# A decoder layer at fp32 accuracy: seven more pairs of gemms through seven block products, and the mixer's constants loaded at other places

## Chip, cores and metric

The kernel runs on one core of one Trainium2 chip. The metric is the device time of one execution in microseconds (us). The profile has five engines: PE (TensorE, with its weight loads as PEld), ACT (ScalarE), DVE (VectorE), POOL (GpSimd) and SP (SyncE, which issues nearly all DMAs).

## The reference

One layer, x of 256 tokens × 2048, all in float32, batch 1:

```python
x = x + 1/2 * SwiGLU_1(rms(x))          # SwiGLU(x) = (silu(x @ w_gate) * (x @ w_up)) @ w_down, D_FF 5632
h = rms(x)
[q | k | v | u | vs | g_att | g_sg] = h @ w_in                # 1536 each for q k v u vs, 2048 each gate
# A: 12 heads of 128, causal dilated windows (128,1) (512,4) (2048,16), partial rotary -> y_att (w_att_out)
# B: u = gelu(u); vs = layernorm(gelu(vs)); y_sg = (u * (W_s vs + b)) @ w_sg_out, W_s lower triangular per group
merged = sigmoid(g_att) * y_att + sigmoid(g_sg) * y_sg
x = x + merged @ w_out
x = x + 1/2 * SwiGLU_2(rms(x))
out = rms(x)
```

## The kernel before

All gemms have 256 rows (two token tiles of 128) and are cut into column blocks of 512; `gemm(w, c0, rows0, nk, lhs, post, group, bank, quad)` puts one such block on a list. The left operand lies in SBUF turned (features on the partitions), the weights stream from HBM.

**Accuracy.** Operands are split into a high and a low part of a reduced type (fp32r): hi is a rounded copy, lo the rest. A product is three matmuls, hi·hi, hi·lo and lo·hi. Weights are split by ACT (L235, `wh`) and DVE (L236, `wl`), 128×1024 at a time.

**Steps.** The list of gemms becomes a list of steps (`lay_out`). A plain step is two rows of 128 of k: one `wh`, one `wl`, 12 matmuls of 128×512. Raw weights come in units of 1 MB (`load_unit`, L181), three buffers deep, each for two plain steps. The main loop issues the matmuls of step i (L243), then the callbacks that are due at its end, then the splits of up to three steps ahead (LA = 3); `wh` and `wl` have four buffers. The order on every engine is the order in which this loop writes the instructions, and an engine does its queue in that order. `at(place, fn)` registers a callback; places count plain steps as 1 and quad steps as 0.5.

**Quads.** Two gemms side by side can do one chunk of four k rows as a 2×2 by 2×2 block product with seven products instead of eight (`quad_products`, forms p1 to p7). Each form is a quad step: six matmuls, one `wh`, one `wl`. Four blocks of raw weights (512 KB each, `load_block`) sit in a room; `prepare` (L211) makes four sums and differences of them on DVE, `sums_of` (L311 to L317) those of the left operand, and three ACT copies and two DVE adds (L292 to L301) put the results together in PSUM. p1, p6 and p7 are done 5, 3 and 1 steps ahead of the end of the gemm before, the others among the first five steps of the pair. Before the change there are 27 quads: nearly all of FFN1 and FFN2. In FFN2 the first pair of gate and up (f = 0) is plain; so is the whole mixer. `CS = 2` is the chunk of x that quads take.

**Turns.** A result that becomes a left operand is turned by `turn`: DVE transposes of 32×32 (L349) into `bt`, a DMA to a buffer in HBM (`bm`, L333), four DMAs back (L339), then `ev`: for x, ACT scales it by the norm's gains (L430) and splits it into `xhi` (ACT, L321) and `xlo` (DVE, L322). For chunk 2 of x0 and x2 `sums_of` follows at once, with its ACT copy (L316) and its lo part (L317). The operands x0, x1, x2 (of FFN1, mixer, FFN2) have four chunks each (`xt1_0` to `xt1_3`: x1's).

**Residuals.** `residual` adds a gemm's result to x (DVE, L411), ACT sums the squares (L377), and the turn of that chunk follows.

**The mixer.** In order: vs and u (three gemms each, gelu, layer norm, the spatial products), q and k, v, attention among them; then for c = 0 to 3 the gate gs (w_in), w_sg_out, ga (w_in), w_att_out and the turn of merged chunk c; then w_out. `mixer_consts` loads the rope table `cs_t`, the attention masks, the spatial weights (`room`) and the layer norm's rows (`ln`), L526 to L546, nine steps ahead of the mixer; two `sgw_turn`s turn the spatial weights 8 and 18 steps into it.

Of the kernel before, what the change touches and what calls it, by code (L numbers as in the profile page):

```python
# [18 lines left out]
P = 128  # L19
# [19 lines left out]
CS = 2  # L39
# [5 lines left out]
def layer(ctx: ExitStack, tc: tile.TileContext, a, out):  # L45
# [138 lines left out]
    def next_of(quad):  # L184
        k = quads.index(quad) + 1
        return quads[k] if k < len(quads) and quads[k]["stage"] is quad["stage"] else None

    def room_for(quad):
        quad["room"] = (big.tile([P, 4, 2, NC], F32, tag="C", name="quads"), big.tile([P, 2, NC], F32, tag="k2", name="sum"),
                        sb.tile([P, 3, NC], F32, tag="W", name="part"))  # L190
        for b in (0, 2, 3, 1):
            load_block(quad, b)

    def load_block(quad, b):
        if quad is None:
            return
        if "room" not in quad:
            quad["room"] = quads[quads.index(quad) - 1]["room"]
# [3 lines left out]
        SP.dma_start(quad["room"][0][:, b], src[:, j])  # L202

    def blocks_of(quad):
        r = quad["room"]
        return [r[0][:, b] for b in range(4)] + [r[1], r[2][:, 1:3], r[2][:, 0]]
# [98 lines left out]
    def sums_of(tag_pool, tag, v, name):  # L305

        v = v.rearrange("p (q m) i b -> p m q i b", m=4)
        a0, a1, b0, b1 = (v[:, m] for m in range(4))
        f = sb.tile([P, 4, 2, P], F32, tag="gate", bufs=2, name=f"fs{name}")
        s1, s2, s3, s4 = (f[:, k].rearrange("p q (i b) -> p q i b", b=32) for k in range(4))  # L310
        DVE.tensor_tensor(s1, a1, b1, op=OP.add)  # L311
        DVE.tensor_tensor(s2, s1, a0, op=OP.subtract)
        DVE.tensor_tensor(s3, a1, a0, op=OP.subtract)
        DVE.tensor_tensor(s4, b0, s2, op=OP.subtract)
        both = tag_pool.tile([P, 2, 4, 2, P], F32R, tag=tag, name=f"fp{name}")
        ACT.activation(both[:, 0], f, AF.Copy)  # L316
        DVE.tensor_tensor(both[:, 1], f, both[:, 0].bitcast(F32), op=OP.subtract)  # L317
        return both[:, 0], both[:, 1]
# [107 lines left out]
    def turn_x(i, n, c, lag, read=3):  # L426
        def evac(src):
# [5 lines left out]
            if c == CS and n != 1:  # L433
                xT["forms"] = sums_of(big, "oT", src, f"x{n}")
# [235 lines left out]
    def post_qk(key, gi):  # L670
        def post(e, banks):
# [58 lines left out]
            if key == "k" and gi == 2:  # L730
                attention(e + 16)
# [374 lines left out]
```

## Time and profile before

| what | value |
|---|---|
| time, median of 3 runs (lowest, highest) | 2026.97 us (2026.89, 2029.02) |
| profiled execution: time, span, granted clock | 2025.94 us, 2024.2 us, 0.997 |
| instructions in it | 24110 |
| bytes moved, mean rate | 471.54 MB, 233 GB/s |
| DMA queue of SP, share of 16 engines | 71.9% |

A row of the groups reads: line, engine, operation, out<-in, shape, count | busy us, mean ns | idle just before, and its releaser. In the timeline the numbers ahead are the start and the duration in us, and brackets hold idle time and its releaser. Matmuls are pipelined, so that a single one's 0.38 us overlaps its neighbours.

### The profile page before, as it was taken

How to read it: one execution, taken by the hardware profiler on the slowest of the kernel's cores; microseconds unless marked ns; L12 is line 12 of the kernel's file. 1: busy time of each engine (PE TensorE's matmuls, PEld its weight loads, DVE VectorE, ACT ScalarE, POOL GpSimd, SP SyncE). 2: the span in 40 equal slices, each digit the busy share in tenths (PEclk: the TensorE clock that was granted, in tenths of full speed). 3: DMA queues.
4: the chain of work that ended last, by engine and by line, in shares of the span. 5: the costliest groups of instructions: out<-in, count | busy, mean ns of one | idle time of the engine just before them, and what ended most of it. 6: DMA issues, size and time to landing. Idle time of an engine off the chain costs nothing.

```text
span 2024.2 us, 24110 instructions
## 1 busy us (share of the span) xinstructions
PE 2002.4 (99%) x9323; PEld 1750.0 (86%) x9323; DVE 1437.0 (71%) x1463; ACT 1105.7 (55%) x1240; POOL 11.3 (1%) x19
## 2 busy tenths in 40 slices
PE   9999999999999899999999999999999999999998
PEld 7888888888888788888888888888888888888887
DVE  6788776778877567675665555677878776787775
ACT  6555645555556455454554444466655554566554
POOL 0000000000000000000000000000000000000000
PEclk9999999999999999999999999999999999999999
DMA  8778776677775876788776666788777766687764
GB/s 313 257 232 249 229 233 214 198 228 232 242 244 183 273 252 204 227 276 267 259 235 216 229 204 216 237 279 253 235 221 239 254 211 192 219 248 229 233 214 142
DMA packets 249499, 471.54 MB, mean 233 GB/s; under 512 B 12460, under 2 KB 41000, under 8 KB 249256
## 3 DMA queue, kind: packets, MB, share of 16 engines
q1 hardware_dynamic: 249064, 469.47, 71.9%
q8 instruction: 73, 1.20, 0.2%
q10 hardware_dynamic: 320, 0.53, 0.1%
q14 instruction: 42, 0.34, 0.1%
HBM read 440.30 MB, written 29.66 MB: 232 GB/s over the span
## 4 chain that ended last, share of the span: by engine, by line
PE 93%; DMA 2%; DVE 2%; ACT 1%; issue 1%; SPq 0%; POOLq 0%; POOL 0%; ACTq 0%; DVEq 0%
PE qd L243 57%; PE mm L243 35%; DMA xt<-bmx 1%; DMA more<-in_ffn_w_gate_dram 1%; DVE wl L236 1%; ACT xt L430 0%; ACT wh L235 0%; DMA raw<-in_ffn_w_down_dram 0%; DMA raw<-in_ffn_w_gate_dram 0%; ACT xhi L321 0%; DVE btx L349 0%; PE sp L646 0%; DMA bmx<-btx 0%; SPq L339 0%; PE pv L812 0%
## 5 line engine op out<-in xcount | busy, mean ns | idle before, releaser
L236 DVE TENSOR_TENSOR wl<-raw,wh 128x1024 fp32r<-128x1024 f32 (+1 forms) x665 | 806.9, 1217 | 411.1 <-ACT wh L235 409.3
L235 ACT ACTIVATE wh<-raw 128x1024 fp32r<-128x1024 f32 (+1 forms) x665 | 696.0, 1051 | 598.4 <-PE mm L243 300.8
L243 PE MATMUL qd<-wh,xhi 128*128 128x512 f32 x1026 | 388.9, 379 | 0.0
L243 PE MATMUL qd<-wl,xhi 128*128 128x512 f32 x1026 | 388.9, 379 | 0.0
L243 PE MATMUL qd<-wh,xlo 128*128 128x512 f32 x1026 | 388.9, 379 | 0.0
L243 PE MATMUL mm<-wh,xhi 128*128 128x512 f32 x928 | 352.6, 380 | 2.2 <-ACT wh L235 1.9
L243 PE MATMUL mm<-wh,xlo 128*128 128x512 f32 x928 | 351.8, 379 | 0.0
L243 PE MATMUL mm<-wl,xhi 128*128 128x512 f32 x928 | 350.0, 379 | 1.7 <-DVE wl L236 1.7
L243 PEld LDWEIGHTS qd<-wl,xhi 128*128 128x128 f32 x1026 | 193.9, 189 | 27.7
L243 PEld LDWEIGHTS qd<-wh,xhi 128*128 128x128 f32 x1026 | 193.9, 189 | 27.7
L243 PEld LDWEIGHTS qd<-wh,xlo 128*128 128x128 f32 x1026 | 193.9, 189 | 27.4
L243 PEld LDWEIGHTS mm<-wh,xhi 128*128 128x128 f32 x928 | 175.4, 189 | 27.8 <-ACT wh L235 2.8
L243 PEld LDWEIGHTS mm<-wl,xhi 128*128 128x128 f32 x928 | 175.4, 189 | 27.1 <-DVE wl L236 2.3
L243 PEld LDWEIGHTS mm<-wh,xlo 128*128 128x128 f32 x928 | 175.4, 189 | 25.0 <-DVE xlo L404 0.3
L235 ACT ACTIVATE wh<-quads 128x1024 fp32r<-128x1024 f32 x108 | 114.0, 1055 | 146.5 <-PE qd L243 141.6
L236 DVE TENSOR_TENSOR wl<-quads,wh 128x1024 fp32r<-128x1024 f32 x108 | 131.4, 1217 | 50.1 <-ACT wh L235 49.3
L243 PE MATMUL qd<-wh,fpx 128*128 128x512 f32 x304 | 102.9, 379 | 1.4 <-DVE qd L301 1.4
L236 DVE TENSOR_TENSOR wl<-sum,wh 128x1024 fp32r<-128x1024 f32 x54 | 66.1, 1225 | 37.0 <-ACT wh L235 35.3
L235 ACT ACTIVATE wh<-sum 128x1024 fp32r<-128x1024 f32 x54 | 57.1, 1057 | 29.2 <-PE qd L243 18.1
L243 PEld LDWEIGHTS qd<-wh,fpx 128*128 128x128 f32 x304 | 57.5, 189 | 9.9 <-ACT wh L235 1.8
L243 PE MATMUL qd<-wh,hhi23.0_663 128*128 128x512 f32 x172 | 65.2, 379 | 0.0
L243 PE MATMUL qd<-wl,hhi23.0_663 128*128 128x512 f32 x172 | 65.2, 379 | 0.0
(402 smaller groups left out, 2366.0 us busy)
## 6 DMA issues: line engine op xcount, KB each, us to landing
raw<-in_w_in_dram SPq DMA_DIRECT2D x92, 1024.0 KB, 5.3
raw<-in_ffn_w_down_dram SPq DMA_DIRECT2D x72, 1024.0 KB, 5.2
raw<-in_ffn_w_gate_dram SPq DMA_DIRECT2D x66, 1024.0 KB, 6.2
raw<-in_ffn_w_up_dram SPq DMA_DIRECT2D x66, 1024.0 KB, 5.8
quads<-in_ffn_w_gate_dram SPq DMA_DIRECT2D x38, 512.0 KB, 5.7
quads<-in_ffn_w_up_dram SPq DMA_DIRECT2D x38, 512.0 KB, 3.6
quads<-in_ffn_w_down_dram SPq DMA_DIRECT2D x32, 512.0 KB, 3.8
raw<-in_w_out_dram SPq DMA_DIRECT2D x16, 1024.0 KB, 5.1
```

The costliest lines, as they stand in the source:

```text
L235: ACT.activation(wh[:, k], r[:, k], AF.Copy)
L236: DVE.tensor_tensor(wl[:, k], r[:, k], wh[:, k].bitcast(F32), op=OP.subtract)
L243: PE.matmul(g["ps"][t], act, in_turn(w), start=not g["begun"][t], stop=g["left"][t] == 0, skip_group_check=g["quad"] is not None)
```

## The change

- Seven more pairs become quads (27 to 34): vs2 with u0, u1 with u2, gs with ga for c = 2 and for c = 3 (so w_sg_out comes behind ga there), w_out's columns 0 and 1, 2 and 3, and gate and up of FFN2's f = 0.
- Rooms are now `home`s, one for each stretch: FFN1, the front of the mixer (`gates`), the second half of the mixer with FFN2's first pair (`merge`), FFN2. Each is moved in at a place of its own: `gates` one step into the mixer.
- `CS` names a chunk for each x: 2, 0, 0. x1 now has forms too; two ACT copies (`keep`) hold them from the first q gemm on for the gates. The merged operand's forms come from its chunk 2 (`CM`).
- `sums_of` is split into two callbacks, the second one step later, everywhere.
- `mixer_consts` falls into three: rope and masks at place 88 (middle of FFN1), spatial weights 7 and layer norm rows 10 steps into the mixer; the turns of the spatial weights at +13 and +21.

```diff
@@ -36,7 +36,8 @@
-CS = 2
+CS = (2, 0, 0)
+CM = 2
...
+    def ffn_home():
+        c = big.tile([P, 4, 2, NC], F32, tag="C", name="quads")
+        k = big.tile([P, 2, NC], F32, tag="k2", name="sum")
+        w = sb.tile([P, 3, NC], F32, tag="W", name="part")
+        return [c[:, b] for b in range(4)] + [k, w[:, 1:3], w[:, 0]]
+    def gate_home():
+        b_ = big.tile([P, 6, 2, NC], F32, tag="B", name="quads")
+        return [b_[:, b] for b in range(6)] + [big.tile([P, NC], F32, tag="k2", name="part")]
+    def merge_home():
+        l_ = sb.tile([P, 3, 2, NC], F32, tag="L", name="quads")
+        k = big.tile([P, 2, NC], F32, tag="k2", name="quads4")
+        w = sb.tile([P, 3, NC], F32, tag="W", name="part")
+        t = sb.tile([P, 2, NC], F32, tag="tmp", bufs=2, name="sum")
+        return [l_[:, b] for b in range(3)] + [k, t, w[:, 1:3], w[:, 0]]
+    def move_in(home):
+        home["room"] = home["make"]()
         for b in (0, 2, 3, 1):
+            load_block(next(q for q in quads if q["home"] is home), b)
...
+    def sums_of(i, store, v, name, tag="gate"):
+        got = {}
+        def sums():
+            w = v.rearrange("p (q m) i b -> p m q i b", m=4)
+            a0, a1, b0, b1 = (w[:, m] for m in range(4))
+            got["f"] = f = sb.tile([P, 4, 2, P], F32, tag=tag, bufs=2, name=f"fs{name}")
+            s1, s2, s3, s4 = (f[:, k].rearrange("p q (i b) -> p q i b", b=32) for k in range(4))
+            DVE.tensor_tensor(s1, a1, b1, op=OP.add)
+            DVE.tensor_tensor(s2, s1, a0, op=OP.subtract)
+            DVE.tensor_tensor(s3, a1, a0, op=OP.subtract)
+            DVE.tensor_tensor(s4, b0, s2, op=OP.subtract)
+        def parts():
+            both = store()
+            split_psum(both[:, 0], both[:, 1], got["f"])
+        at(i, sums)
+        at(i + 1, parts)
+    def forms_tile(pool, tag, name, keep):
+        def store():
+            keep["forms"] = pool.tile([P, 2, 4, 2, P], F32R, tag=tag, name=name)
+            return keep["forms"]
+        return store
+    def forms_in(keep):
+        return lambda: (keep["forms"][:, 0], keep["forms"][:, 1])
...
-            if c == CS and n != 1:
-                xT["forms"] = sums_of(big, "oT", src, f"x{n}")
+            if c == CS[n]:
+                sums_of(i + lag, forms_tile(big, "oT", f"fx{n}", xT), src, f"x{n}")
+    homes = []
+    merge = dict(make=merge_home)
-        sides[0] = 0
+        home = dict(make=ffn_home)
+        homes.append(home)
...
-                            st["forms"] = sums_of(sb, "L", src, f"h{e}")
+                            sums_of(e + 10, forms_tile(sb, "L", f"fh{e}", st), src, f"h{e}")
-                if f == 0 or f == 1 and group is FIRST:
-                    bank = tp_bank if f == 1 or group is PAIR else mm_bank
+                if f < 2 and group is FIRST:
+                    bank = tp_bank if f == 1 else mm_bank
-                quad = dict(chunk=CS, forms=lambda: xT["forms"], stage=wd)
-                gemm(wg, f * NC, 0, KD, lhs_x, post_gate, BOTH, bank, quad)
+                n = 0 if group is FIRST else 2
+                quad = dict(chunk=CS[n], forms=forms_in(xT), home=home if f or not n else merge)
+                gemm(wg, f * NC, 0, KD, lhs_x, post_gate, BOTH if f else PAIR, bank, quad)
-                    quad = dict(chunk=0, forms=lambda st=st: st["forms"], stage=wd)
+                    quad = dict(chunk=0, forms=forms_in(st), home=home)
...
-    def mixer_consts():
+    def masks():
...
+    def spatial_weights():
         SP.dma_start(raw.rearrange("p (g s) -> p g s", g=NG), a["sg_w"][0].rearrange("g t s -> t g s"))
+    def layer_norm_rows():
         ln = sb.tile([P, 2, SGW], F32, tag="L", name="ln")
...
-                parts = big.tile([P, 4, one], F32R, tag="A", name="qk0")
+                parts = mix["A"] = big.tile([P, 6, one], F32R, tag="A", name="qk0")
+                mix["forms"] = parts[:, 4:6].rearrange("p h (f q t) -> p h f q t", f=4, q=2)
+                kept = xT["forms"]
+                def keep():
+                    for h in range(2):
+                        ACT.activation(mix["forms"][:, h], kept[:, h].bitcast(F32), AF.Copy)
+                at(e + 4, keep)
...
+                at(e + 16 + 15 + 12, lambda: move_in(merge))
...
-                mix["mhi"] = big.tile([P, KD, S], F32R, tag="A", name="mhi")
+                mix["mhi"] = mix["A"][:, 0:4].rearrange("p a (k s) -> p (a k) s", s=S)
-            turn(e + 2, f"m{c}", 8, put_tokens(lambda: ga), lambda: flat(ga),
-                 lambda src: split_psum(turned(mix["mhi"][:, 4 * c:4 * c + 4]),
-                                        turned(mix["mlo"][:, 4 * c:4 * c + 4]), src))
+            def ev(src):
+                split_psum(turned(mix["mhi"][:, 4 * c:4 * c + 4]), turned(mix["mlo"][:, 4 * c:4 * c + 4]), src)
+                if c == CM:
+                    sums_of(e + 10, lambda: mix["forms"], src, "m", "tmp")
+            turn(e + 2, f"m{c}", 8, put_tokens(lambda: ga), lambda: flat(ga), ev)
-    for j in range(3):
-        gemm(w_in, o_s + j * NC, 0, KD, lhs_x, post_gelu("vs", j), PAIR if j == 0 else (1, None))
-    for j in range(3):
-        gemm(w_in, o_u + j * NC, 0, KD, lhs_x, post_gelu("u", j))
+    gates = dict(make=gate_home)
+    front = [(o_s + j * NC, post_gelu("vs", j)) for j in range(3)] + [(o_u + j * NC, post_gelu("u", j)) for j in range(3)]
+    for j, (c0, post) in enumerate(front):
+        if j < 2:
+            gemm(w_in, c0, 0, KD, lhs_x, post, PAIR if j == 0 else (1, None))
+            continue
+        if j % 2 == 0:
+            bank = side()
+            quad = dict(chunk=CS[1], forms=forms_in(xT), home=gates)
+        gemm(w_in, c0, 0, KD, lhs_x, post, BOTH, bank, quad)
+    sg_out = lambda: (mix["uT"][:, 0], mix["uT"][:, 1])
+    att_out = lambda: (mix["oT"][:, 0], mix["oT"][:, 1])
-        gemm(w_in, o_gs + c * NC, 0, KD, lhs_x, post_sig("gs"))
-        gemm(a["w_sg_out"][0], c * NC, 0, NG, lambda: (mix["uT"][:, 0], mix["uT"][:, 1]), post_mul("gs"))
-        gemm(w_in, o_ga + c * NC, 0, KD, lhs_x, post_sig("ga"))
-        gemm(a["w_att_out"][0], c * NC, 0, NSLOT, lambda: (mix["oT"][:, 0], mix["oT"][:, 1]), post_merge(c))
+        if c < 2:
+            bank = (mm_bank, tp_bank)[c]
+            gemm(w_in, o_gs + c * NC, 0, KD, lhs_x, post_sig("gs"), bank=bank)
+            gemm(a["w_sg_out"][0], c * NC, 0, NG, sg_out, post_mul("gs"), bank=bank)
+            gemm(w_in, o_ga + c * NC, 0, KD, lhs_x, post_sig("ga"), bank=bank)
+        else:
+            sides[0] += c == 2
+            bank = side()
+            quad = dict(chunk=CS[1], forms=forms_in(mix), home=merge)
+            gemm(w_in, o_gs + c * NC, 0, KD, lhs_x, post_sig("gs"), BOTH, bank, quad)
+            gemm(w_in, o_ga + c * NC, 0, KD, lhs_x, post_sig("ga"), BOTH, bank, quad)
+            gemm(a["w_sg_out"][0], c * NC, 0, NG, sg_out, post_mul("gs"), bank=bank)
+        gemm(a["w_att_out"][0], c * NC, 0, NSLOT, att_out, post_merge(c), bank=bank)
+        if c % 2 == 0:
+            bank = side()
+            quad = dict(chunk=CM, forms=forms_in(mix), home=merge)
-             lambda e, banks, c=c: residual(e, 2, c, banks, 1.0, True), PAIR if c == 0 else (1, None))
+             lambda e, banks, c=c: residual(e, 2, c, banks, 1.0, True), PAIR if c == 0 else BOTH, bank, quad)
...
-    at(mixer - 9, mixer_consts)
+    at(88, masks)
+    at(mixer + 7, spatial_weights)
+    at(mixer + 10, layer_norm_rows)
-        sgw_turn(mixer + 8 + 10 * h, h)
+        sgw_turn(mixer + 13 + 8 * h, h)
-    for after, stage in ((12, a["ffn1_w_gate"][0]), (start_of(ffn2_gate) + 1, ffn2_gate)):
-        at(after, lambda: room_for(next(q for q in quads if "room" not in q)))
+    for after, home in ((12, homes[0]), (mixer + 1, gates), (start_of(ffn2_gate) + 1, homes[1])):
+        at(after, lambda home=home: move_in(home))
```

The rest of the diff passes `home` instead of `stage` and `room_for`. The order of the instructions moves in three places that matter here. First SP, around the second turn of x1 just ahead of the mixer (`bmx1_1` to HBM, `xt1_1` back). Before:

```order
L333 DMA bmx1_1_5029<-btx1_1_5026 128x1024
L181 DMA raw104_5041<-in_ffn1_w_down_dram 128x4x512
L526 DMA cs_t_85<-in_rope_cs_dram 128x128
L532 DMA mask_rows_5076<-in_att_mask_dram 64x3x128
...
L546 DMA ln_5089<-in_sg_ln_b_dram 128x1536
L339 DMA xt1_1_5092<-bmx1_1_5029 32x4x256 x4
```

After:

```order
L362 DMA bmx1_1_5045<-btx1_1_5042 128x1024
...
L368 DMA xt1_1_5094<-bmx1_1_5045 32x4x256 x4
L182 DMA raw105_5099<-in_ffn1_w_down_dram 128x4x512
L182 DMA raw106_5137<-in_w_in_dram 128x4x512
L362 DMA bmx1_2_5164<-btx1_2_5161 128x1024
L182 DMA raw107_5182<-in_w_in_dram 128x4x512
L368 DMA xt1_2_5216<-bmx1_2_5164 32x4x256 x4
...
L217 DMA quads_5297<-in_w_in_dram 128x2x512 x4
...
L362 DMA bmx1_3_5333<-btx1_3_5330 128x1024
L182 DMA raw111_5351<-in_w_in_dram 128x4x512
```

The constants stood between the two DMAs of the turn; now the way back follows one raw unit, and the four blocks of `gates` (L217) stand between the turns of chunks 2 and 3.

DVE at the start, around the sums of x0's chunk 2 (`fsx0`, then their lo part). Before:

```order
L322 TENSOR_TENSOR xlo0_127<-xt0_2_331,xhi0_126 128x1024
L311 TENSOR_TENSOR fsx0_403<-xt0_2_331 128x256
...
L314 TENSOR_TENSOR fsx0_403<-xt0_2_331,fsx0_403 128x256
L317 TENSOR_TENSOR fpx0_408<-fsx0_403,fpx0_408 128x1024
L236 TENSOR_TENSOR wl14_414<-raw7_313,wh14_413 128x1024
```

After (`fx0` is the lo part):

```order
L351 TENSOR_TENSOR xlo0_127<-xt0_2_331,xhi0_126 128x1024
L328 TENSOR_TENSOR fsx0_403<-xt0_2_331 128x256
...
L331 TENSOR_TENSOR fsx0_403<-xt0_2_331,fsx0_403 128x256
L250 TENSOR_TENSOR wl14_411<-raw7_313,wh14_410 128x1024
L351 TENSOR_TENSOR fx0_433<-fsx0_403,fx0_433 128x1024
```

The weights' `wl` has come ahead of the lo part; on ACT the same holds for `wh` and the hi part.

DVE at the end of w_out, from p4 of its second quad on: x2's first chunk is evacuated and, now, summed there. Before, the chunk's split stood alone:

```order
L236 TENSOR_TENSOR wl541_9979<-raw225_9892,wh541_9978 128x1024
L236 TENSOR_TENSOR wl542_9995<-raw225_9892,wh542_9994 128x1024
L236 TENSOR_TENSOR wl543_10013<-raw226_9937,wh543_10012 128x1024
L322 TENSOR_TENSOR xlo2_9888<-xt2_0_9971,xhi2_9887 128x1024
L349 STREAM_TRANSPOSE btx2_1_10034<-x_81 128x4x4x32 x2
L236 TENSOR_TENSOR wl544_10040<-raw226_9937,wh544_10039 128x1024
L236 TENSOR_TENSOR wl545_10058<-raw227_9976,wh545_10057 128x1024
```

After (L225 is `prepare` for FFN2's first quad, `quads_8248` and `quads4_8249` its blocks):

```order
L250 TENSOR_TENSOR wl561_10143<-sum_8251,wh561_10142 128x1024
L225 TENSOR_TENSOR part_8250<-quads_8248 128x1024
L250 TENSOR_TENSOR wl562_10160<-raw214_9999,wh562_10159 128x1024
L351 TENSOR_TENSOR xlo2_10021<-xt2_0_10108,xhi2_10020 128x1024
L328 TENSOR_TENSOR fsx2_10175<-xt2_0_10108 128x256
...
L331 TENSOR_TENSOR fsx2_10175<-xt2_0_10108,fsx2_10175 128x256
L225 TENSOR_TENSOR quads_8248<-quads_8248,quads4_8249 128x1024
L250 TENSOR_TENSOR wl563_10184<-raw215_10058,wh563_10183 128x1024
L378 STREAM_TRANSPOSE btx2_1_10199<-x_81 128x4x4x32 x2
L351 TENSOR_TENSOR fx2_10204<-fsx2_10175,fx2_10204 128x1024
L250 TENSOR_TENSOR wl564_10208<-quads_8248,wh564_10207 128x1024
L225 TENSOR_TENSOR sum_8251<-quads4_8249,part_8250 128x1024
```

Between the `wl`s now stand four sums, three prepares and the forms' lo part `fx2`.

More of the change, by code (lines that the diff above doesn't have):

```diff
@@ L185, in next_of @@
         k = quads.index(quad) + 1
[L186 to L190, printed above, removed]
+        return quads[k] if k < len(quads) and quads[k]["home"] is quad["home"] else None
+    def ffn_home():
[14 more added lines that the diff above has]
+        home["room"] = home["make"]()
         for b in (0, 2, 3, 1):
-            load_block(quad, b)
+            load_block(next(q for q in quads if q["home"] is home), b)
     def load_block(quad, b):
@@ L303, in quad_products @@
         close(g, i)
[L305 to L318, printed above, removed]
+    def sums_of(i, store, v, name, tag="gate"):
[21 more added lines that the diff above has]
+        return lambda: (keep["forms"][:, 0], keep["forms"][:, 1])
     def split_psum(hi, lo, src):
```

7 lines of the change are left out of this document (2 added, 5 removed).

## The prediction

> **What bounds the kernel now.** I read the engines' busy time first, then PE's waits, the windows, and the chain of work that ended last.
>
> ```profile
> PE 2002.4 (99%) x9323; PEld 1750.0 (86%) x9323; DVE 1437.0 (71%) x1463; ACT 1105.7 (55%) x1240; POOL 11.3 (1%) x19
> ...
> L236 DVE TENSOR_TENSOR wl<-raw,wh 128x1024 fp32r<-128x1024 f32 (+1 forms) x665 | 806.9, 1217 | 411.1 <-ACT wh L235 409.3
> ...
> L235 ACT ACTIVATE wh<-quads 128x1024 fp32r<-128x1024 f32 x108 | 114.0, 1055 | 146.5 <-PE qd L243 141.6
> ```
>
> PE is busy for 99% of the span: matmuls are the time, and only fewer of them, or fewer waits of PE, can move it. DVE, at 71%, is the only other engine that could take over. PE's waits, as line waited for, total, times, longest:
>
> ```profile
> PE qd L243 <- ACT wh L235: 5.2, 2, 4.7
> PE mm L243 <- ACT wh L235: 1.9, 1, 1.9
> PE qd L243 <- DVE wl L236: 1.8, 1, 1.8
> PE mm L243 <- DVE wl L236: 1.7, 2, 1.0
> PE qd L243 <- DVE qd L301: 1.4, 1, 1.4
> ```
>
> They sum to 12.0 us, and one of 4.7 stands out. The windows place it (columns: busy PE, PEld, DVE, ACT, POOL, granted clock, DMA share, GB/s):
>
> ```profile
> 40.00:50.00 10.00, 7.16 (x33) 5.71 (x32) 6.90 (x11) 7.21 (x11) 0.33 (x1) 1.00 0.63 208
> 500.00:600.00 100.00, 100.00 (x465) 87.58 (x464) 79.36 (x76) 57.59 (x61) 0.00 (x0) 1.00 0.74 237
> 600.00:700.00 100.00, 92.99 (x419) 80.12 (x419) 64.88 (x66) 55.05 (x75) 3.50 (x6) 0.97 0.70 226
> 672.00:690.00 18.00, 11.48 (x43) 9.04 (x42) 9.40 (x9) 10.28 (x15) 0.00 (x0) 0.81 0.85 283
> 760.00:770.00 10.00, 10.00 (x48) 8.77 (x47) 9.28 (x11) 3.87 (x5) 0.00 (x0) 1.00 0.63 211
> 900.00:1300.00 400.00, 400.00 (x1901) 351.63 (x1900) 236.51 (x252) 192.29 (x212) 0.00 (x0) 1.00 0.72 232
> ```
>
> Where FFN1 runs by block products (500:600), DVE is busy 79% and PE never waits. In the mixer (900:1300) DVE is at 59%, ACT at 48%. The hole is at the mixer's start.
>
> **Removed: matmuls.** The chain gives the time per matmul while nothing is waited for:
>
> ```profile
> 108.30 515.66 PE qd L243 x2388
> ...
> 663.64 9.66 DMA xt<-bmx
> 673.48 1.71 ACT xt L430 x4
> ...
> 689.48 129.50 PE mm L243 x600
> ...
> 1342.11 4.11 DMA xt<-bmx
> ```
>
> 515.66/2388 and 129.50/600 both give 0.216 us (the 0.38 of single rows overlaps). A quad does a chunk of two gemms in 42 matmuls instead of 48. Seven quads: 42 × 0.2157 = **−9.1 us**. Bytes stay: 28 loads of 512 KB replace 14 of 1 MB.
>
> **Removed: the hole at the mixer's start.** SP's queue and PE's rows there:
>
> ```profile
> 655.21 0.37 SPq L181 DMA_DIRECT2D raw<-in_ffn_w_down_dram  x1
> 655.63 0.55 SPq L526 DMA_DIRECT2D cs_t<-in_rope_cs_dram  x1
> ...
> 661.65 0.34 SPq L546 DMA_DIRECT2D ln<-in_sg_ln_b_dram  x1
> 662.04 2.34 SPq L339 DMA_DIRECT2D xt<-bmx  x4
> ```
>
> ```profile
> 672.21 0.38 PE L243 MATMUL qd<-wh,hlo157.0_3275 128*128 128x512 f32 x1
> 677.27 0.79 PE L243 MATMUL qd<-wh,hhi157.0_3274 128*128 128x512 f32 x1 [4.68 <-ACT wh L235]
> 679.90 0.79 PE L243 MATMUL qd<-wl,hhi157.0_3274 128*128 128x512 f32 x1 [1.84 <-DVE wl L236]
> ...
> 683.48 0.40 PE L243 MATMUL qd<-wh,hhi157.0_3274 128*128 128x512 f32 x1
> ...
> 689.10 0.38 PE L243 MATMUL qd<-wh,hlo157.0_3275 128*128 128x512 f32 x1
> ```
>
> The view names ACT's `wh`, but ACT itself stood behind the evacuation of `xt` (673.48), which waited for its transfer, and SP issued that behind the constants' eight DMAs, 6.4 us after cs_t. The transfer then took 9.66 us beside them, 4.11 elsewhere. From 672.21 to 689.10 PE does 36 matmuls, worth 7.8 us, in 16.9: 9.1 lost, of which 6.5 are the two waits; 679.90 to 683.48 holds eight matmuls 0.45 apart, 1.9 more than at 0.216, and the rest is the slow first ones. With the constants elsewhere, `xt` is issued as soon as bmx is written and lands some 8 us sooner; 6.6 us (673.3 to 679.90) separate landing from the hl product, which PE reaches at 672.4, so 7.5 us would do. I take **−9.1**; since that is near, up to 3 may remain.
>
> **Removed: three sums.** The operand's sums now stand one step behind, as two callbacks, so the next step's `wh` and `wl` go first.
>
> ```profile
> 43.73 1.06 ACT L316 ACTIVATE fpx<-fsx 128x1024 fp32r<-128x1024 f32 x1 [2.76 <-DVE fsx L314]
> ```
>
> ```profile
> 43.53 0.38 PE L243 MATMUL mm<-wh,xlo 128*128 128x512 f32 x1
> 45.79 0.48 PE L243 MATMUL mm<-wh,xhi 128*128 128x512 f32 x1 [1.88 <-ACT wh L235]
> 47.23 0.48 PE L243 MATMUL mm<-wl,xhi 128*128 128x512 f32 x1 [0.96 <-DVE wl L236]
> ...
> 108.30 0.45 PE L243 MATMUL qd<-wh,fpx 128*128 128x512 f32 x1 [1.44 <-DVE qd L301]
> ...
> 642.56 0.45 PE L243 MATMUL qd<-wh,fph157.0_3495 128*128 128x512 f32 x1 [0.49 <-ACT wh L235]
> ...
> 1360.45 0.48 PE L243 MATMUL mm<-wl,xhi 128*128 128x512 f32 x1 [0.78 <-DVE wl L236]
> ```
>
> At the start ACT waits 2.76 us for DVE (a lo part of 1.22, then four sums, so 1.54 for these) while the next `wh` stands behind it. From 43.53 to 47.23 PE does two matmuls' time of work in 3.7: 3.4 lost. In the new order `wh` is done before the sums end; `wl` still follows them on DVE, so that the hl product comes about 1.2 after 43.7 where hh has filled 0.2: some 1.0 stays, **−2.4**. The sums of FFN1's first h (1.44) go, **−1.4**; those of x2 leave that place, **−0.8**. Bounds: nothing to these rows. Removed in all: 22.8.
>
> **Added: work beside PE.** Further durations:
>
> ```profile
> L211 DVE TENSOR_TENSOR sum<-quads,part 128x1024 f32<-128x1024 f32 x27 | 32.9, 1219 | 0.0
> L301 DVE TENSOR_TENSOR qd<-qd,part 128x512 f32<-128x512 f32 x27 | 18.7, 693 | 0.0
> L349 DVE STREAM_TRANSPOSE btx<-x 128x512 f32<-128x512 f32 x20 | 13.0, 687 | 0.0
> L295 ACT ACTIVATE part<-qd 128x512 f32<-128x512 f32 x27 | 16.1, 595 | 5.7 <-PE qd L243 5.7
> L317 DVE TENSOR_TENSOR fpx<-fsx,fpx 128x1024 fp32r<-128x1024 f32 x2 | 2.4, 1224 | 2.2 <-ACT fpx L316 2.2
> ```
>
> A quad takes three more splits (1.22 on DVE, 1.06 on ACT), four prepares (1.22 each) and two adds (0.69) on DVE, three copies (0.59) on ACT. Seven: DVE 7 × (3.66 + 4.88 + 1.38) = 69, and two new sets of sums make about 75; ACT 7 × 4.95 = 35, and with the two copies that keep the x1 forms 39. Average cover is ample: the mixer, from 690 to 1335, has 41% of DVE idle, some 260 us. Locally the splits run at most three steps (6 to 7 us of PE) ahead, and that lead has to carry each peak. So the price is read stage by stage, by counting DVE's rows in the new order against PE's steps (2.59 plain, 1.295 of a quad); the lead takes what it can:
>
> - x1's new sums and their lo part (1.54 + 1.22) go into the two steps of x1_0's evacuation, ten steps behind a place that is already late (642.56). The lead takes some 1.9 of 2.8: **+0.9**.
> - The second quad of the front (u1/u2) runs under layer norm, the stage of the row 760:770 with DVE already at 93%. Ten steps, p7 to p4, hold on DVE ten `wl` (12.2), twelve layer-norm operations (8.3 by L301's duration, the same shape), a prepare, two adds and a split of the spatial weights (4.6): 25.1 against 20.7 of PE. The lead carries about 4: **+0.5**.
> - w_out's first pair, with chunk 2 taken out as a quad, uses chunk 3 of the merged operand sooner: by the order the turned chunk comes one plain step (2.6) ahead of its use, and between stand on ACT a copy, a `wh` and the hi part (0.6 + 1.06 + 1.06), on DVE the lo part (1.22), 3.9: **+1.2**.
> - p3 of w_out's second quad waits for x's adds, then `wh`, `wl`, the add of L301: the row of 0.49 is the same queue: **+0.55**.
> - w_out's last gemm: x2_0's evacuation, its four sums (1.55), three prepares, a transpose and both parts of fx2 fall in six steps. DVE's rows there: six `wl` 7.3, three prepares 3.7, two lo parts 2.4, sums 1.54, transposes 1.4, in all 16.4; PE has four plain and two quad steps, 13.0. Behind the wait just told little of the lead is left, some 0.6: **+2.8**, and **+0.45** where the next x adds (1.4) join the late queue.
> - p3 of FFN2's first quad: again the queue of 642.56 (0.49), with x2_2's lo part (1.22) in it as well: **+1.7**, near the 1.44 at 108.30.
>
> Together **+8.1**. No row of before has these stacks, so the bounds are 0, if each finds its lead (row 500:600: 79% with no wait), and 15, if each finds none. I stay near the middle, since rows on both sides (0.00 at 500:600; 0.49, 1.44) stand for the same queues.
>
> **Moved, at no cost.** Rope and masks go into FFN1, five issues on SP (3.4 us at 655.63) with DMA shares of 0.74 around and `raw` buffered three units ahead; if the cover went, 1 us. The gates' four blocks (2 MB, 7.4 us at the 283 GB/s of 672:690) wait in SP's queue until FFN1's last product frees their tile; behind them stand one raw and x1_3's turn, to whose evacuation ACT comes eight steps (21 us) later. Spatial weights follow six steps (15 us) ahead of their first turn, layer-norm rows some 20 steps ahead of use. The copies that keep x1's forms (two of 1.06) find ACT at 48%. The merge and FFN2 blocks come while gemms run at share 0.72. Nothing for these; 0 to 3 together.
>
> **Sum.** −9.1 − 9.1 − 4.6 + 8.1 = −14.7 on a span of 2024.2: 2009.5. The profiled execution took 2025.94, 1.74 around its span, and stands 1.0 under the median of 2026.97: **2012.3**, and I forecast 2012.5.
>
> **The rivals.**
> 1. The hole moves instead of going. The gates' 2 MB and two raws take the constants' place and delay x1_2 or x1_3. For: DMA share 0.85 at 672:690. Against: these transfers are issued behind xt1_1 and xt1_2. Price 9.1: about 2021.5.
> 2. The new stacks find their lead, as in 500:600, since a whole lead of 6 to 7 us would hold any one of them, and each was charged with a lead already part used: 2012.5 − 8 = 2004.5.
> 3. Slower: DVE becomes the bound in the quads' stages. Mechanism: with 9.9 us more per quad, DVE's row 760:770 would stand above 10 of 10, each `wl` comes late, `wh` and `raw` buffers free late, SP follows. It decides when over 22.8 us, a third of the added 75, shows on PE; half of it, 37, gives 2004.5 + 37 = 2041. Against: the quads' 79% at 500:600 shows none.
> 4. The clock. After 4.68 idle the matmuls took 0.79 (twice 0.38), and the clock was 0.81 in 672:690; after 1.88 and 0.96 (40:50) it stayed 1.00. The edge lies between. Should the waits of w_out's last gemm come as one (2.8 + 0.45), and those of w_out's start and FFN2's with others, each pays the 1.9 of half clock and one more split: two such, 2017. The Trainium skill, "TensorE: Matmul & The Clock Gate", section "HAM oscillation — how this bites in real kernels", lets the clock fall back after idle gaps over about 3.4 us. Both rows agree with it, and by it a wait of 3.25 would just escape; without it the chance stays the same.
>
> **Chances.** My forecast, 2007 to 2018, 0.62; rival 2, 0.12; rival 1, 0.10; the clock, 0.08; DVE, 0.08. What this measurement can tell is 0.2%, 4 us: faster is below 2022.9, slower above 2031.0. Forecast, rivals 2 and 4 and half of rival 1 are faster: 0.87. The rest of rival 1 and a mild DVE case make 0.07; slower 0.06. Range 2004 to 2021.5: rival 2 below, rival 1 above; out stay DVE and tails.
>
> **What would show it.** Right: 42 matmuls fewer; no ACT wait of 4 us at the mixer's start, clock 1.00 there; PE's wait near 45 about 1 us; a few waits of 0.5 to 3 between 1290 and 1370 on `wl` and on the add that ends q12. Wrong: an `xt` transfer on the chain near 690; DVE at 95% or more over 50 us with PE under 97%; any matmul of 0.79 after 50.

## The result, and the profile after

The changed kernel took 2015.86 us, median of four runs (2015.27 to 2016.67), against 2027.99 of the kernel before in the same comparison (2026.89 to 2029.44): ratio 0.994, 95% interval 0.9923 to 0.9957. The forecast was 2012.5, range 2004 to 2021.5. The profiled execution has a span of 2014.9 against 2024.2. So the direction stands, and the time lies in the range: 12.1 us were gained where 14.5 were forecast. The ledger behind it does not stand, as the experiments show: what was removed came out somewhat larger than forecast, and the seven quads, forecast as a small gain, are a loss.

The page and PE's waits of the changed kernel (line waited for, total, times, longest):

```profile
PE 1996.0 (99%) x9281; PEld 1741.1 (86%) x9281; DVE 1505.2 (75%) x1536; ACT 1141.1 (57%) x1286; POOL 11.2 (1%) x19
```

```profile
PE qd L257 <- DVE wl L250: 4.6, 4, 3.1
PE qd L257 <- ACT wh L249: 2.2, 3, 1.2
PE pv L854 <- ACT vq L798: 1.0, 1, 1.0
...
PE qd L257 <- DVE mlo L351: 0.8, 1, 0.8
...
```

42 matmuls are gone, and DVE has 73 instructions and 68 us more. The single wait of 4.7 on ACT is gone, but four waits on `wl`, the longest 3.1, have come. The windows (columns as before) show where:

```profile
672.00:690.00 18.00, 18.00 (x85) 15.77 (x84) 11.10 (x14) 11.17 (x16) 0.70 (x1) 1.00 1.04 376
760.00:780.00 20.00, 18.74 (x84) 15.25 (x83) 19.86 (x24) 13.29 (x18) 0.00 (x0) 1.00 0.48 158
...
1135.00:1171.00 36.00, 36.00 (x169) 31.52 (x168) 27.08 (x26) 18.93 (x19) 0.00 (x0) 1.00 0.74 239
...
1320.00:1330.00 10.00, 6.90 (x24) 5.42 (x24) 10.00 (x13) 3.90 (x4) 0.00 (x0) 0.83 0.14 55
```

The mixer's start is full, and so is the first of the gates' quads (1135:1171, DVE at 75%). Under the layer norm (760:780) and at the end of w_out (1320:1330) DVE is at 99 to 100% while PE waits; and in 1320:1330 the clock is 0.83.

**The hole at the mixer's start.** SP's queue, then the chain:

```profile
651.21 0.34 SPq L362 DMA_DIRECT2D bmx<-btx  x1
653.46 0.37 SPq L182 DMA_DIRECT2D raw<-in_ffn_w_down_dram  x1
653.93 3.14 SPq L368 DMA_DIRECT2D xt<-bmx  x4
```

```profile
656.63 6.30 DMA xt<-bmx
663.09 1.72 ACT xt L459 x4
```

The way back follows the way out by 2.7 us instead of 7.9, the transfer takes 6.3 instead of 9.66, and ACT evacuates at 663.1, 10.4 earlier. Of these 10.4, all rows there have moved by 4.4 (the wait of 642.56 stands at 638.20 now); the other 6.0 are the turn's own.

**The new waits.** PE's timeline (start, duration, idle and releaser in brackets), the start of the kernel first:

```profile
44.02 0.38 PE L257 MATMUL mm<-wh,xhi 128*128 128x512 f32 x1
44.53 0.48 PE L257 MATMUL mm<-wl,xhi 128*128 128x512 f32 x1
...
653.48 0.48 PE L257 MATMUL qd<-wl,hhi157.0_3285 128*128 128x512 f32 x1 [0.58 <-DVE wl L250]
...
775.51 0.48 PE L257 MATMUL qd<-wl,xhi 128*128 128x512 f32 x1 [0.73 <-DVE wl L250]
...
1285.65 0.48 PE L257 MATMUL qd<-wh,mlo 128*128 128x512 f32 x1 [0.75 <-DVE mlo L351]
...
1307.98 0.46 PE L257 MATMUL qd<-wh,qk 128*128 128x512 f32 x1 [0.49 <-ACT wh L249]
...
1355.16 0.46 PE L257 MATMUL qd<-wh,fx 128*128 128x512 f32 x1 [1.18 <-ACT wh L249]
```

The start now loses 0.3 where it lost 3.3 (0 to 1.2 in the profiles of the runs below that have the split sums). The other five rows stand at five of the six places that the prediction named; the sixth, the end of w_out, follows. From here on a loss is the distance of two matmuls' starts less 0.216, so that 1.18 idle counts 1.34; the loss of a stretch is the sum over all its matmuls.

**The end of w_out**, the largest: the stretch from 1317 to 1337 loses 5.6 us, 1.6 of them in seven matmuls at half clock. PE, then DVE, ACT and SP:

```profile
1319.71 0.38 PE L257 MATMUL qd<-wh,qk 128*128 128x512 f32 x1
1323.15 0.80 PE L257 MATMUL qd<-wl,qk 128*128 128x512 f32 x1 [3.06 <-DVE wl L250]
...
1326.30 0.38 PE L257 MATMUL qd<-wh,mlo 128*128 128x512 f32 x1
```

```profile
1306.00 1.23 DVE L250 TENSOR_TENSOR wl<-quads,wh 128x1024 fp32r<-128x1024 f32 x1 [1.96 <-ACT wh L249]
...
1318.14 1.23 DVE L351 TENSOR_TENSOR xlo<-xt,xhi 128x1024 fp32r<-128x1024 f32 x1 [3.50 <-ACT xhi L350]
...
1321.88 1.22 DVE L250 TENSOR_TENSOR wl<-raw,wh 128x1024 fp32r<-128x1024 f32 x1
```

```profile
1315.31 1.71 ACT L459 ACTIVATE xt<-xt,gcols 128x256 f32<-128x256 f32 x4 [2.11 <-DMA xt<-bmx]
```

```profile
1301.77 0.34 SPq L362 DMA_DIRECT2D bmx<-btx  x1
...
1307.26 0.37 SPq L217 DMA_DIRECT2D quads<-in_ffn_w_up_dram  x1
1307.72 1.84 SPq L368 DMA_DIRECT2D xt<-bmx  x4
```

Read it backwards. PE wants the `wl` that DVE begins at 1321.88, behind `xlo`, the sums and a prepare. But DVE was idle for 3.5 us ahead of `xlo`: ACT evacuated late, because the transfer came late, because SP issued it 5.9 us after the way out. Ahead of it in SP's queue stood the load of a block for FFN2's first quad, which waits for the split that frees its room (1306.00 to 1307.23), and that split waits for its `wh`, which ACT does behind the sums of squares of the residual's adds. So the stack that I had counted on DVE has a queue of SP in it that I had not; run 4 tests it.

### The profile page after: what moved, and what is told of

Read it like the earlier page. It is cut to its first block, busy times and chain, and to the rows that moved or that the text cites. A ratio compares the mean times of both kernels' runs of the same rounds, so it can differ in the third digit from the quotient of the medians.

```text
span 2014.9 us, 24165 instructions
## 1 busy us (share of the span) xinstructions
PE 1996.0 (99%) x9281; PEld 1741.1 (86%) x9281; DVE 1505.2 (75%) x1536; ACT 1141.1 (57%) x1286; POOL 11.2 (1%) x19
## 3 DMA queue, kind: packets, MB, share of 16 engines
q8 instruction: 72, 1.18, 0.2%
## 4 chain that ended last, share of the span: by engine, by line
PE 87%; DMA 5%; DVE 4%; ACT 2%; issue 2%; SPq 1%; POOLq 0%; POOL 0%; ACTq 0%; DVEq 0%
PE qd L257 67%; PE mm L257 18%; DMA xt<-bmx 2%; DVE wl L250 2%; ACT wh L249 1%; DMA bmx<-btx 1%; DMA uroom<-bmu 1%; ACT xt L459 1%; DMA raw<-in_w_in_dram 1%; DMA p<-bmp 1%; SPq L368 1%; DVE btx L378 0%; ACT junk L406 0%; ACT xhi L350 0%; DVE xlo L351 0%
## 5 line engine op out<-in xcount | busy, mean ns | idle before, releaser
L257 PE MATMUL qd<-wl,xhi 128*128 128x512 f32 x1296 | 491.4, 379 | 0.7 <-DVE wl L250 0.7
L257 PE MATMUL qd<-wh,xhi 128*128 128x512 f32 x1296 | 491.2, 379 | 0.0
L257 PE MATMUL qd<-wh,xlo 128*128 128x512 f32 x1296 | 491.2, 379 | 0.0
L257 PE MATMUL mm<-wh,xhi 128*128 128x512 f32 x608 | 231.1, 380 | 0.2 <-ACT xhi L432 0.2
L257 PE MATMUL mm<-wh,xlo 128*128 128x512 f32 x608 | 230.5, 379 | 0.0
L257 PE MATMUL mm<-wl,xhi 128*128 128x512 f32 x608 | 228.8, 380 | 0.6 <-DVE wl L250 0.4
L257 PEld LDWEIGHTS mm<-wl,xhi 128*128 128x128 f32 x608 | 114.9, 189 | 17.9 <-DVE wl L250 1.8
L257 PE MATMUL qd<-wh,fx 128*128 128x512 f32 x352 | 119.3, 380 | 1.7 <-ACT wh L249 1.2
L257 PEld LDWEIGHTS qd<-wh,fx 128*128 128x128 f32 x352 | 66.5, 189 | 12.2 <-ACT wh L249 1.6
L257 PE MATMUL qd<-wl,fx 128*128 128x512 f32 x176 | 66.8, 380 | 0.0
```

The lines of the kernel that those rows point to most:

```text
L257: PE.matmul(g["ps"][t], act, in_turn(w), start=not g["begun"][t], stop=g["left"][t] == 0, skip_group_check=g["quad"] is not None)
```

## Experiments

Each kernel is told as its edit against the kernel before or the changed one. Theory A says that each wait belongs to an order in a queue at its place, so that the parts of the change add up; the rivals, that waits only move (B), or that transfers are slow in themselves (C). Runs 1, 2, 4 and 5, runs 3 and 6 to 8, and runs 9 to 11 were timed in three groups, each with the kernel before beside them (2026.12, 2028.23 and 2027.64), so that across groups the ratios tell more than the times.

**1. The constants alone**, on the kernel before (its `mixer_consts` is cut in three as in the change).

```diff
-    at(mixer - 9, mixer_consts)
+    at(88, masks)
+    at(mixer + 7, spatial_weights)
+    at(mixer + 10, layer_norm_rows)
-        sgw_turn(mixer + 8 + 10 * h, h)
+        sgw_turn(mixer + 13 + 8 * h, h)
```

> The kernel before with one part of the change alone: the rope table and masks loaded in the middle of FFN1, the spatial weights 7 and the layer norm's rows 10 steps into the mixer, their turns at +13 and +21. Theory A (the hole at the mixer's start is SP's queue: the constants stand ahead of the transfer xt1_1): the waits of 4.68 and 1.84 us near 677 go, with the half clock behind them, 9.1 us in all, so a span near 2015 and a time near 2019 against 2028. Rival (the transfer is late beside raw weights anyway, or the hole moves to x1_2 or x1_3 and the late constants make one of their own): 3 us or less, 2025 to 2028.

Measured: 2016.46 against 2026.12, ratio 0.9951 (0.9939 to 0.9964); span 2014.7, 9.5 less. PE's waits:

```profile
PE mm L243 <- DVE wl L236: 2.3, 3, 1.0
PE qd L243 <- DVE qd L301: 1.4, 1, 1.4
```

No wait near 677 is left: the stretch 672 to 690 lost 9.1 us before and loses nothing here. (By chance the start loses 1.3 less than in the profile before, and a wait near 865 takes 0.8.) The whole hole goes with this one edit, and it alone gives the span of the whole change. Where, then, had nine us of matmuls gone?

**2. The constants back**, on the changed kernel.

```diff
-    at(88, masks)
-    at(mixer + 7, spatial_weights)
-    at(mixer + 10, layer_norm_rows)
+    at(mixer - 9, masks)
+    at(mixer - 9, spatial_weights)
+    at(mixer - 9, layer_norm_rows)
...
-        sgw_turn(mixer + 13 + 8 * h, h)
+        sgw_turn(mixer + 8 + 10 * h, h)
```

> The changed kernel with the constants loaded again nine steps ahead of the mixer and the turns at +8 and +18. Theory A: the hole comes back in full or nearly, 6 to 10 us: a time of 2022 to 2026 against 2015.9. Rival (the other edits, the split sums and the front's quads, have changed the place so far that the transfer is early or late for other reasons): within 3 us of the changed kernel. If theory A holds, this and the run with the constants alone give the same 9 us from both sides.

Measured: 2023.95 (ratio 0.9988 to the kernel before, 0.9979 to 0.9997), span 2022.2. The hole is back:

```profile
675.52 0.79 PE L257 MATMUL qd<-wh,hhi157.0_3274 128*128 128x512 f32 x1 [6.91 <-ACT wh L249]
```

It is deeper than in the kernel before: 11.5 us are lost there, not 9.1. The span grows by 7.3 only, since other rows lose less: under the layer norm one wait of 0.5 is left of three, and two rows of the changed kernel's profile, near 863 and 1002, do not come. By the times the edit costs 8.1 us, by the ratios 9.7.

**3. Constants and split sums, without any of the seven quads**, on the kernel before: the edit of 1 and

```diff
-                xT["forms"] = sums_of(big, "oT", src, f"x{n}")
+                sums_of(i + lag, big, "oT", src, f"x{n}", xT)
...
+        at(i, sums)
+        at(i + 1, parts)
```

> The kernel before with two parts of the change and none of its seven quads: the constants loaded at the later places, and the operand's sums split into two callbacks, one step apart. The constants alone gave a span of 2014.7, as short as the whole change (2014.9). Theory A (the split takes the start's 2.0 us of waits to 0.3, the 1.6 of FFN1's first h to nothing and x2's 1.35 to about 0.3): span 2010 to 2011, time near 2012, so that the seven quads, for all their 42 matmuls fewer (9.1 us), cost 4 us net in the changed kernel. Rival (the split only moves these waits one step on): 2013 to 2015, and the quads come out at about nothing.

Measured: 2011.18 against 2028.23, ratio 0.9917 (0.9904 to 0.9931), span 2008.8. In the main loop one wait is all that remains:

```profile
PE qd L243 <- ACT wh L235: 0.5, 1, 0.5
```

This is the central finding. These two parts of the change make the kernel about 17 us faster; with the seven quads added it takes 2015.86 (2014.8 in run 11). The quads, with 9.1 us of matmuls less, cost 3.6 to 4.7 us net by the medians, 4.5 to 4.7 by the ratios. The intervals of the ratios overlap a little (0.9904 to 0.9931 against 0.9923 to 0.9957); the traces say the same, with losses of 6.0 us over all matmuls here and 20.8 in the changed kernel.

**4. Two neighbours in SP's queue exchanged**, on the changed kernel: x2_0's way back ahead of the block's load.

```diff
-        turn_x(e + (6 if c == 1 else 2), n, c, 6)
+        turn_x(e + (6 if c == 1 else 2), n, c, 6, 1 if (n, c) == (2, 0) else 3)
```

> The changed kernel with two neighbours in SP's queue exchanged: the way back of x2_0's turn stands ahead of the load of a block for FFN2's first quad, which waits for a split behind the residual's adds. Nothing else moves. Theory A (the 3.06 us wait near 1320 begins with that load: the way back was issued 5.9 us after its way out, and ACT idled 2.1 us for it): the way back goes out some 1.5 to 2 us earlier, the wait falls to about 1 to 1.5 us, and with it the seven matmuls at half clock behind it (1.5 us) go: 3 to 4 us, a span of 2011. Rival B (DVE has 16.4 us of rows for 13.0 of matmuls there, whenever the chunk lands): the wait stays at 2.5 to 3 us. Rival C (the transfer is slow because the DMA engines are at their limit there, share 1.00): it lands as late as before.

Measured: 2013.2 against 2026.12, ratio 0.993 (0.9917 to 0.9944), span 2011.7, 3.2 less than the changed kernel; by the times 1.6 to 2.7 less, with intervals that overlap. SP and PE:

```profile
1303.87 1.75 SPq L368 DMA_DIRECT2D xt<-bmx  x4
...
1306.28 0.39 SPq L217 DMA_DIRECT2D quads<-in_ffn_w_up_dram  x1
```

```profile
1319.97 0.48 PE L257 MATMUL qd<-wl,qk 128*128 128x512 f32 x1 [0.85 <-DVE wl L250]
...
1323.42 0.48 PE L257 MATMUL qd<-wl,xhi 128*128 128x512 f32 x1 [0.60 <-DVE wl L250]
...
1325.69 0.48 PE L257 MATMUL qd<-wl,qk 128*128 128x512 f32 x1 [0.71 <-DVE wl L250]
```

The way back goes out 3.1 us after the way out instead of 5.9, and ACT evacuates at 1312.13 instead of 1315.31: the transfer was late for its place in the queue, not in itself (C falls here). The end of w_out loses 3.4 us instead of 5.6, and the half clock is gone; what else the span gained lies elsewhere, mostly in the row near 1002. The three waits shown still lose 2.6. That is near the 2.8 that the prediction counted on DVE, but DVE still idles for 1.28 ahead of `xlo`, so that DVE's count need not be all of it.

**5. x2's sums behind the next `wl`**, on the changed kernel (sums half a place later, in a buffer of another pool).

```diff
-                sums_of(i + lag, forms_tile(big, "oT", f"fx{n}", xT), src, f"x{n}")
+                sums_of(i + lag + (n == 2) / 2, forms_tile(big, "oT", f"fx{n}", xT), src, f"x{n}", "tmp" if n == 2 else "gate")
```

> The changed kernel with the four sums of x2_0 behind the next weights' low part and the transposes of x2_1, and the forms' low part behind one more split; the way back of the turn stays where it is. Theory A (order: sums of 1.5 us stand ahead of the low part that the waiting matmul needs): the 3.06 us wait near 1320 falls by 1.5 to 1.6 us, and the half clock behind it goes (1.5 us): about 3 us, span 2012. Rival B (load: the rows only come later): the wait at the place falls, but new waits of the same sum, 1.5 to 3 us, show in the next five steps, and the time stays within 1 us of the changed kernel.

Measured: 2016.78, ratio 0.995 (0.9938 to 0.9963), span 2015.0: nothing gained; the end of w_out loses 6.6 us. The wait of 3.06 became three:

```profile
1320.52 0.48 PE L257 MATMUL qd<-wl,qk 128*128 128x512 f32 x1 [1.25 <-DVE wl L250]
...
1324.31 0.48 PE L257 MATMUL qd<-wl,xhi 128*128 128x512 f32 x1 [0.94 <-DVE wl L250]
...
1327.80 0.48 PE L257 MATMUL qd<-wl,qk 128*128 128x512 f32 x1 [1.92 <-DVE wl L250]
...
1328.80 0.63 PE L257 MATMUL qd<-wl,qk 128*128 128x512 f32 x1
```

Here B is right. With DVE's start as late as before, the other order only changed which matmul waits; the half clock came too (0.63 at 1328.80). Starting earlier (4) helps, shuffling does not.

**6. FFN2's first pair plain**, on the changed kernel.

```diff
-CS = (2, 0, 0)
+CS = (2, 0, 2)
-                if f < 2 and group is FIRST:
-                    bank = tp_bank if f == 1 else mm_bank
+                if f == 0 or f == 1 and group is FIRST:
+                    bank = tp_bank if f == 1 or group is PAIR else mm_bank
```

> The changed kernel with one of the seven quads undone: gate and up of FFN2's f = 0 are plain again, and x2's sums come from chunk 2 as before. Six matmuls more, 1.3 us. Theory A (this quad alone makes the stack at w_out's end: waits of 3.2, 0.4, the half clock 1.5, small ones 0.7, and 1.3 at its p3, 7.1 us in all; of it some 0.5 returns for x2's sums in their old place): a span of 2008.5 to 2010, five to six less. Rival B (DVE is loaded there by w_out's own quad, x2_0 comes late anyhow): 2 to 4 us of the waits stay, span 2012 to 2014.

Measured: 2017.29, ratio 0.9947 (0.9935 to 0.996), span 2013.7. A miss, and neither theory's: the waits at the end of w_out are gone, as A said, but a new hole stands at x2_2's sums. DVE, then PE:

```profile
1347.09 0.43 DVE L328 TENSOR_TENSOR fsx<-xt 128x256 f32<-128x256 f32 x1 [4.37 <-DMA bmx<-btx]
```

```profile
1349.84 0.79 PE L257 MATMUL mm<-wl,xhi 128*128 128x512 f32 x1 [4.79 <-DVE wl L250]
```

With w_out's last two gemms done side by side, x2_3's transposes come ahead of x2_2's sums, and their buffer is the one that the sums want. A wait on a buffer stood in DVE's queue with a `wl` behind it; with the half clock the place loses 8.0 us. Run 9 tests the buffer.

**7. The front's two quads plain**, on the changed kernel.

```diff
-        if j < 2:
+        if j < 6:
...
-    for after, home in ((12, homes[0]), (mixer + 1, gates), (start_of(ffn2_gate) + 1, homes[1])):
+    for after, home in ((12, homes[0]), (start_of(ffn2_gate) + 1, homes[1])):
```

> The changed kernel with two quads undone, vs2 with u0 and u1 with u2; x1's sums stay, for the gates. Twelve matmuls more, 2.6 us. Theory A (these two pay back 0.4 + 0.4 + 0.9 at single waits and some 0.6 in small ones under the layer norm): within 1 us of the changed kernel, span 2014 to 2016. Rival (these waits come from the layer norm and the spatial weights' turns, at any rate, since the kernel with the constants alone has one of 0.7 near 864): they stay, span 2017 or more.

Measured: 2017.82, ratio 0.9948 (0.9936 to 0.9961), span 2015.2. Under the layer norm no wait is left:

```profile
760.00:780.00 20.00, 20.00 (x95) 17.50 (x94) 17.19 (x21) 13.02 (x19) 0.00 (x0) 1.00 0.68 223
```

So the waits there were these quads': DVE 19.86 of 20 with them, 17.19 without. In span they are worth about what they cost. The runs were 2 us slower than the changed kernel's, with ratios whose intervals overlap. In the profile the gain is taken back in FFN2: its p3 waits 2.56 instead of 1.18, and the clock falls once more there. The chain to that wait begins with x2_2's way back. In the changed kernel, in this run and in run 11, which is the changed kernel again:

```profile
1341.32 4.60 DMA xt<-bmx
```

```profile
1338.36 5.89 DMA xt<-bmx
```

```profile
1339.47 5.62 DMA xt<-bmx
```

The waits are 1.18, 2.56 and 2.18. So p3's wait is long where this transfer is long, and the changed kernel has it without any edit: the edit of this run need not be its cause. (Runs 2 and 4 fit, with 4.74 and 4.42 us and waits of 1.31 and 1.05; run 5, with 5.00 and 1.05, does so less.) Here theory C fits. Why the transfer's time varies is not shown.

**8. Six quads, x1's sums two steps later**: the edit of 6, and

```diff
-                sums_of(i + lag, forms_tile(big, "oT", f"fx{n}", xT), src, f"x{n}")
+                sums_of(i + lag + 2 * (n == 1), forms_tile(big, "oT", f"fx{n}", xT), src, f"x{n}", "tmp" if n == 1 else "gate")
```

> As the kernel with FFN2's first pair plain, and x1's four sums two steps later, behind the transposes of x1_1, with their parts one more step on; six quads stay. Theory A: besides the 5 to 6 us of that kernel, the waits of 0.74 and 0.40 to 0.95 near 652 and 669 go: a span near 2008, the shortest of all. Rival B: the sums only collide with the steps that follow; no difference from the kernel with FFN2's first pair plain.

Measured: 2016.07, ratio 0.9936 (0.9922 to 0.9949), span 2015.5, where A said 2008. The waits near 652 and 669 are gone as A said (1.1 us in the changed kernel), but the hole of 6 is here as well, 1.0 deeper: no gain over 6 can be told from this run.

**9. The same, and another buffer for x2's sums.** In the line of 8:

```diff
-"tmp" if n == 1 else "gate")
+"tmp" if n else "gate")
```

> As the kernel with six quads (FFN2's first pair plain, x1's sums later), with x2's sums in a buffer of another pool. There the sums of x2_2 waited 4.4 us, by the timeline, for the DMA that still read their buffer as the turn of x2_3, and PE 4.8 to 5.8 for the low part behind them, with some 2.4 us of half clock after it. Theory A (that buffer is the whole of it): the hole of 6.4 and the half clock go, 8 to 9 us, span 2006 to 2007.5, two under the kernel with constants and sums alone (2008.8), so that six quads in better places gain some 2 us net. Rival B (load at the end of w_out): another wait of 2 to 4 us takes its place, span 2009 to 2011, and the quads gain nothing even so.

Measured: 2008.26 against 2027.64, ratio 0.9905 (0.9891 to 0.9918); spans 2005.6 to 2008.5 over its runs. PE's waits on `wl` in plain steps (`mm`), in run 8 and here:

```profile
PE mm L257 <- DVE wl L250: 6.4, 2, 5.8
```

```profile
PE mm L257 <- DVE wl L250: 2.2, 4, 1.0
```

The hole and its half clock are gone with the buffer. (The profiled execution was the longest of the four; its longest wait, 1.0, stands at the kernel's start.) This is the shortest time, 6.5 us under the changed kernel of the same group (run 11), with intervals apart, 7.6 under its first time, and faster than both kernels of the case. It is 2.9 under constants and sums alone, with intervals that overlap, so that a gain of six quads over none is likely and not certain.

**10. Four quads**: the edits of 9 and 7 together.

> As the kernel with six quads and the buffer of their own, with the front's two quads (vs2 with u0, u1 with u2) plain: four quads stay, gs with ga and w_out. Theory A (each wait belongs to its place): twelve matmuls more, 2.6 us, against waits of 0.42, 0.42, 0.89 and small ones of 0.3 to 0.6 under the layer norm, 2.0 to 2.4: within 1 us of the kernel with six quads. Rival (their waits would come in any case): 2.6 us slower.

Measured: 2008.26 again, ratio 0.9909 (0.9894 to 0.9924), span 2006.2. Its waits in the main loop:

```profile
PE qd L257 <- ACT wh L249: 1.0, 2, 0.5
...
PE qd L257 <- DVE mlo L351: 0.8, 1, 0.8
PE mm L257 <- DVE wl L250: 0.3, 1, 0.3
```

The front's two quads gain nothing that these runs can tell: against their 2.6 us of matmuls stand their waits, 2.3 us under the layer norm and at times some near 707 (run 11).

**11. The changed kernel again**, without an edit.

> The changed kernel itself, for a second profile and for a comparison on the same chip. Theory A: the waits near 652, 669, 765 to 775, 1284, 1307, 1320 and 1354 come again within 0.3 us each, since they follow from the order; the one before the probability product near 1002 (1.2 us), which no other run of these edits has shown, need not. Span 2013 to 2015. Against a theory that the waits are chance of the transfers, in which other places would show them.

Measured: 2014.8 (2014.53 to 2017.62), ratio 0.9939 (0.9926 to 0.9951), span 2015.9. The waits near 653, 765 to 775, 1283, 1306, 1320 and 1353 are back, the first five within 0.25 us in what they lose. The last loses 1.0 more, and ten matmuls at a lower clock follow it:

```profile
1354.33 0.45 PE L257 MATMUL qd<-wh,fx 128*128 128x512 f32 x1 [2.18 <-ACT wh L249]
```

The row near 669 is not there, and one that loses 0.7 stands near 707; the 1.2 near 1002 is not. So the first profile has about 1.9 us of chance (near 863 and 1002), this one some 2.7 at FFN2's p3, and the other spans of this kernel here are 2012.8 to 2013.7. The wait near 707 comes in four of the eight profiles of kernels with the front's quads (0.4 to 1.2 us lost) and in none without; its chain goes back to x1_3's turn, which SP issues behind the gates' four blocks.

## Why the prediction was right, and where it was not

In the three sums of the prediction, by spans: before 2024.2, constants alone 2014.7, with sums 2008.8, with quads 2014.9.

- **Hole**: forecast −9.1, measured −9.5 in span (1), of which the place itself is 9.1, and +7.3 the other way (2). Right, with its mechanism; nothing of the 3 that might have remained.
- **Sums**: forecast −4.6, measured −5.9 (3 against 1): 2.1 at the start (forecast 2.4), 1.6 for FFN1's h (1.4), 1.2 for x2's (0.8), and 0.8 near 865 that was chance in 1. The forecasts for FFN1's h and x2 were low, since I took the idle time in brackets, and what PE loses is the distance of the starts.
- **Quads**: forecast −9.1 + 8.1 = −1.0, measured +6.1 in this profile, of which 1.9 is chance, and +3.6 to 4.7 in the medians. The matmuls are as counted. The failed step is the new waits. By stretch, with the forecast in brackets: x1's sums 1.4 (0.9); under the layer norm 2.3, and 0.4 near 707 (0.5); w_out's start 1.3 (1.2); its second p3 0.7 (0.55); the end of w_out 5.6 (3.25); FFN2's p3 1.4 (1.7); in all 13.1 (8.1). The places were all right. Two sizes were wrong. Under the layer norm I gave the lead 4 us; its operations take 0.74 to 0.75 where I took 0.69, so that the same count gives 25.8 us on DVE against 20.7 on PE, and with 2.3 lost the lead gave some 2.8, by this estimate. At the end of w_out I counted DVE alone; "moved, at no cost" covered the new loads in SP's queue, and one of them stood ahead of x2_0's way back, worth 2.2 us (4).
- **Luck**: the sum was −14.7 in span, and −9.3 was measured in the profiles, −12.1 in the medians. The removed terms came out 1.7 us better than forecast, and the quads' term some 5 to 7 worse and with the other sign. That the time still lies in the range owes something to these opposite errors and to the width of the range, and does not bear out the ledger.
- **Rivals**: the first (the hole moves) is refuted by 1 and 2 as a price of 9.1; a small piece of it is the wait near 707. The second (all leads hold) is wrong. The third, DVE as the bound, did not decide for the whole: some 13 us show, where its condition was 22.8. But it is its mechanism that eats the 9.1 of matmuls. The fourth, the clock, happened once in this profile and twice in run 11. Its price does not follow from its terms: two times 1.9 + 1.22 on 2012.5 give 2018.7, not 2017.
- **Signs**: those of being right came, with the start's wait at 0.3 instead of 1. Two of being wrong came too: a matmul of 0.80 at 1323.15, and an `xt` transfer on the chain at 693.58 (6.24 us), behind which PE lost only 0.4, near 707.

## What to carry to other kernels

Price the parts of a change apart, and measure them apart: here a minor edit hid that the main one loses. Fewer matmuls bring time only where the engine that prepares them has slack in that stage; under the layer norm, with DVE at 99%, two block products gained nothing; beside the gates, with DVE at 75%, two brought no wait at all. And where an instruction waits in a queue, ask what the next one in it serves: a load that waits for a buffer ahead of a transfer cost 2.2 us of PE's time, and a shared buffer 6 to 8.

## What the runs showed of the hardware

The prediction left the edge of TensorE's clock between waits of 1.88 and 4.68 us. The runs show falls inside that range: after one wait of 3.06 us (0.80 for the first matmul, full speed at 1326.30), of 3.17 and 2.56 in run 7, of 2.82 and 2.18 in run 11. The first row is run 11's stretch with the 2.18, the second that of run 5, where the clock fell after 1.25, 0.94 and 1.92 within 9 us:

```profile
1350.00:1360.00 10.00, 7.82 (x29) 6.21 (x29) 8.07 (x11) 6.19 (x9) 0.69 (x1) 0.83 0.76 274
```

```profile
1320.00:1330.00 10.00, 6.62 (x24) 5.08 (x25) 9.96 (x14) 3.43 (x4) 0.00 (x0) 0.91 0.21 67
```

In run 4 waits of 0.85, 0.60 and 0.71 in the same stretch left it at 1.00. But neither the longest wait nor the idle share of a stretch orders all these rows: at the start of the kernel before, 1.88 and 0.96 within 3.7 us left the clock at 1.00 (the prediction's row 40:50), while run 11's single 2.18 did not. What decides is not shown by these runs. The Trainium skill, "TensorE: Matmul & The Clock Gate", section "HAM oscillation — how this bites in real kernels", speaks of idle gaps over about 3.4 us: the measured gaps of 2.2 to 3.2 after which the clock fell differ from it, and decide. Each fall cost 1.6 to 3.1 us.
